# A hybrid decoder block: the second group of input columns on the shifted input, scale sums by a product with ones, later modulation queued behind

## The chip, the cores and the metric

The kernel runs on one core of a Trainium2 chip. The metric is the time on the device in microseconds (us) of one execution; lower is better. The engines of the core run side by side, each through its own queue in order, and wait for one another by semaphores: TensorE (PE, with its weight loads shown as PEld), VectorE (DVE), ScalarE (ACT), GpSimd (POOL) and SyncE (SP), which issues most of the loads. SBUF and PSUM are the memories on the chip.

## The reference

One layer of a decoder block on 512 positions of width 2048, in float32:

```python
mod = silu(c) @ w_ada + b_ada                      # 6 x 2048
shift1, scale1, gate1, shift2, scale2, gate2 = split(mod)
h = rms_norm(x, norm1_w) * (1 + scale1) + shift1
proj = h @ w_in                                    # 2048 x 7168
aq, ak, av, gq, gf, gi, gg = split(proj)           # 3 x 1024 for attention, 4 x 1024 for HGRN2
attn = rms_norm(dilated_attention(rope(rms_norm(aq)), rope(rms_norm(ak)), av), attn_out_norm_w)
f = lb + (1 - lb) * sigmoid(gf);  q = silu(gq) * 128 ** -0.5
hg = rms_norm(hgrn2(q, f, gi)) * silu(gg)
x = x + gate1 * (concat(attn, hg) @ w_out)
h2 = rms_norm(x, norm2_w) * (1 + scale2) + shift2
x = x + gate2 * (square(relu(h2 @ w_ff1)) @ w_ff2)
```

The case is about the first lines: the six modulation vectors are a product of one row with a matrix of 2048 x 12288, which has to be read from HBM in full, and nothing of `proj` can be finished before `scale1` and `shift1` are known.

## The kernel before

**Layout.** The width of 2048 is cut into 16 channel tiles of 128 (`NK`), the positions into four tiles of 128. The normalised input is kept transposed: `xnT[k]` holds channel tile k, 128 channels by 512 positions. For matmuls each operand is split into a high part, rounded to the matmul's format, and a low part with the rest: `hhi[k]`, `hlo[k]` for the input, `whi`, `wlo` for a weight tile (ACT makes the high part, DVE the low part, lines 35 to 41). A product is three matmuls: hi by whi, lo by whi, hi by wlo (`ch_mm` and `tok_mm`, lines 194 to 208).

**Modulation.** `gemv` (lines 116 to 131) computes a row of a vector-matrix product on DVE: it loads 16 slices of 128 channels, multiplies each by a column of the vector and adds it to one of two accumulators, even and odd slices apart. Each step of the generator is one load of 256 KB, with one slice of 512 columns or two slices of 256. What is left is a sum over the 128 partitions. `to_cols` (lines 138 to 152) does it by transposing each 128 columns of the accumulators on PE and adding up the transposed rows on ACT (a copy with an accumulated output), which gives the result as a column of 128 channels. With 512 columns the two accumulators are added first (line 143); with 256 both are transposed side by side. `mod_cols` (lines 160 to 170) adds the bias on DVE (line 167), and for a scale also forms `(scale + 1) * norm weight` (line 169).

**The first two column groups.** `first_groups` (lines 285 to 298) runs two channel tiles at a time and makes six blocks of 128 output columns: four of the forget gate f and two of the HGRN2 query. It is called for columns 4096 to 4607 with 3072 to 3327, and then for 4608 to 5119 with 3328 to 3583. In the first call `scale_block` computes the scale of the next two channel tiles (blocks of 256 columns) and then scales two tiles: `scaled` (lines 329 to 334) makes `xnT[k]` times `g1c`, from that its high part, from both the low part. The input is not shifted yet. Its shift is added afterwards, since (h + shift) @ w = h @ w + shift @ w: `shift_through` (lines 741 to 755) is one more `gemv`, of the shift vector with the weight columns, and adds the result to f or to the query as a bias. So both groups run on the scaled input alone. Beside the second group `shift_block` takes eight background steps per two tiles for the four shift blocks of 512 columns, and as soon as a block of four tiles has its shift, `shifted` (lines 336 to 339) puts it into `hhi`, `hlo` of these tiles, once the second group has read them. All later projections read the shifted input.

**Order.** The instructions of these stages are put in order when the program is built, for each engine: an instruction that is traced earlier goes first among those that are ready, by the builder's own estimate of time. `tc.issue_after(ins)` puts what a block traces on the engine of `ins` behind `ins` in that engine's queue; it binds no other engine, and no load on SP unless `ins` is on SP. From line 828 on, PE runs in the order of the program text (`manual_schedule`).

**After the two groups** come the projection of the HGRN2 values (line 830, `hv0`), during which the background steps of the two corrections at columns 4096 and 3072 run, and then the others. The queue `bgw` of background generators is: four shift blocks, the correction of f0, the correction of all four heads of `hq0`; then `later`: the correction of f1, the rows of gate1, and the scale and shift columns of the second modulation. `bg_step` advances the first generator in the queue by one step.

**Buffers.** Early loads and long-lived tiles share the pool `io` of 30 buffers (`slot`): x, `xnT`, the loads of the early `gemv`, and the copies of the results f and gq (`keep`, lines 733 to 739). PSUM has four banks with the tag `mm` and four with `bg`; the two query blocks of a group and the transposes of `to_cols` share the latter.

Of the kernel before, what the change touches and what calls it, by code (L numbers as in the profile page):

```python
# [8 lines left out]
F32 = mybir.dt.float32  # L9
# [6 lines left out]
P = 128  # L16
# [28 lines left out]
def hybrid_block(ctx, tc, x, c, positions, norm1_w, w_ada, b_ada, w_in, q_norm_w, k_norm_w,  # L45
# [28 lines left out]
    mhalf = const.tile([P, 32], F32, name="mhalf")  # L74
    pool.memset(mhalf, -0.5)

# [39 lines left out]
    def gemv(view, vec, col0, n=512, early=False):  # L116

        accs = [(work("acc") if early else gv.tile([P, 512], F32, name="acc"))[:, 0:n] for _ in range(2)]
        nk = 512 // n
        for k0 in range(0, NK, nk):  # L120
            raw = spare.pop(0) if early and spare else slot("araw") if early else gv.tile([P, 512], F32, name="araw", bufs=4)
            raw = raw.rearrange("p (k n) -> p k n", n=n)
            nc.sync.dma_start(raw, view[:, k0:k0 + nk, col0:col0 + n])
            for k in range(k0, k0 + nk):
                acc = accs[k % 2]
                if k < 2:
                    dve.tensor_scalar(acc, raw[:, k - k0], vec[:, k:k + 1], None, op0=ALU.mult)
                else:
                    dve.scalar_tensor_tensor(acc, raw[:, k - k0], vec[:, k:k + 1], acc, op0=ALU.mult, op1=ALU.add)  # L129
            yield  # L130
        gemv.acc = accs

    def run_all(g):
        for _ in g:
            pass
        return gemv.acc

    def to_cols(accs, dst):

        nb = accs[0].shape[1] // P  # L140
        parts = 1 if nb == 4 else 2
        if parts == 1:
            dve.tensor_tensor(accs[0], accs[0], accs[1], op=ALU.add)
        yield
        pc = bank("pc")
        for j in range(nb):
            for u in range(parts):
                c = (j * parts + u) * P
                pe.transpose(pc[:, c:c + P], accs[u][:, j * P:(j + 1) * P], ident)
        for j in range(nb):  # L150
            c = pc[:, j * parts * P:(j + 1) * parts * P]
            act.activation(c, c, AF.Copy, accum_out=dst[:, j:j + 1])

# [5 lines left out]

    def mod_cols(kind, b, dst, nw, n=512, early=False):  # L160

        for _ in gemv(ada_v, sc, kind * D + b * n, n, early):
            yield
        nb = n // P
        d = dst[:, b * nb:(b + 1) * nb]
        yield from to_cols(gemv.acc, d)
        dve.tensor_tensor(d, d, bcol[:, kind * NK + b * nb:kind * NK + (b + 1) * nb], op=ALU.add)
        if nw is not None:
            mod_cols.last = dve.scalar_tensor_tensor(d, d, 1.0, nw[:, b * nb:(b + 1) * nb], op0=ALU.add, op1=ALU.mult)
        yield  # L170
# [73 lines left out]

    first_scale = mod_cols(1, 0, g1c, n1c, 256, True)
    for _ in range(8):
# [18 lines left out]
    run_all(first_scale)  # L265
    second_scale = mod_cols(1, 1, g1c, n1c, 256, True)
    spare.extend(hp.tile([P, 512], F32, name="araw", tag=f"{c}{k}") for k in range(8, NK) for c in ("hi", "lo"))
# [32 lines left out]
    def scale_block(k0):  # L300
        if k0 == 0:
            run_all(second_scale)
        elif k0 < 14:
            run_all(mod_cols(1, k0 // 2 + 1, g1c, n1c, 256, True))
        for k in (k0, k0 + 1):
            scaled(k)

    def shift_start(k0):
        if k0 == 14:
            for _ in range(12):  # L310
                bg_step()

    shift_done, behind = set(), []

    def shift_gen(b):
        yield from mod_cols(0, b, s1c, None, 512, True)
        shift_done.add(b)

    def shift_block(k0):
        behind.extend((k0, k0 + 1))  # L320
        for _ in range(8):
            bg_step()
        while k0 == NK - 2 and len(shift_done) < 4:
            bg_step()
        for k in [k for k in behind if k // 4 in shift_done]:
            shifted(k)
            behind.remove(k)

    def scaled(k):
        for l, t in zip((hhi, hlo), pair(k)):  # L330
            l.append(t)
        act.activation(xnT[k], xnT[k], AF.Copy, scale=g1c[:, k:k + 1])
        act.copy(hhi[k], xnT[k])
        dve.tensor_tensor(hlo[k], xnT[k], hhi[k].bitcast(F32), op=ALU.subtract)

    def shifted(k):
        act.activation(hhi[k], xnT[k], AF.Identity, bias=s1c[:, k:k + 1])
        act.activation(xnT[k], xnT[k], AF.Identity, bias=s1c[:, k:k + 1])
        dve.tensor_tensor(hlo[k], xnT[k], hhi[k].bitcast(F32), op=ALU.subtract)

# [207 lines left out]
    def forget(hd, src, f, bias=0.0):  # L548
        act.activation(f, src, AF.Sigmoid, bias=bias)
        dve.tensor_scalar(f, f, omlb[:, hd:hd + 1], lb[:, hd:hd + 1], op0=ALU.mult, op1=ALU.add)  # L550

    def hgrn_q(ht):
        qb = project(3072 + ht * 512, ch_mm)
        qs = []
        for h in range(4):
            q = slot("gq")
            with tc.high_priority():
                act.copy(q, qb[h])
            qs.append(q)
        for q in qs:  # L560
            sg = wk.tile([P, 512], F32, name="sg", tag="ev", bufs=2)
            act.activation(sg, q, AF.Tanh, scale=0.5)
            dve.tensor_scalar(sg, sg, 0.5 * QS, 0.5 * QS, op0=ALU.mult, op1=ALU.add)
            dve.tensor_tensor(q, q, sg, op=ALU.mult)
        return qs
# [174 lines left out]

    def shift_through(col0):

        yield from gemv(win_v, s1c, col0, early=col0 < 4096 + 512)
        col = sm.tile([P, 8], F32, name="scol", bufs=2)
        yield from to_cols(gemv.acc, col[:, 0:4])
        for h in range(4):
            if col0 == 3072:
# [4 lines left out]
            else:  # L752
                f, hd = ((f0, h), (f1, 4 + h))[(col0 - 4096) // 512]
                forget(hd, f[h], f[h], col[:, h:h + 1])
# [76 lines left out]
    while bgw:  # L831
        bg_step()
    bgw[:] = later
    tasks.append(hgrn(f0, hq0, hv0, hrs[0]))
# [20 lines left out]
    def project_out(q, rate, after):  # L855
# [16 lines left out]
        return banks  # L872

    def nothing(i):
        pass

# [503 lines left out]
```

## Time and profile before

| what | us |
|---|---|
| median of three runs | 2305.67 |
| lowest and highest of the three | 2302.22, 2305.82 |
| the profiled execution | 2306.17 |
| its span in the profile | 2304.4 |
| matmuls (PE) busy | 2230.5 |
| VectorE busy | 1825.9 |
| ScalarE busy | 1103.0 |

The span is the time from the first to the last instruction that the profile shows; the execution's own time holds a little more. Busy times of engines overlap, so they don't add up to the span. Matmuls are pipelined: one lasts longer than the distance to the next one, and a PE that is busy throughout isn't always at its peak. A row of a timeline gives the start, the length and the engine of an instruction or of a few like ones in a row, its line, what it writes and reads and, in brackets, the idle time before it with what ended it. L12 is line 12 of the kernel.

### The profile page before, as it was taken

The page shows a single profiled execution, that of the slowest core. Times are in us where ns is not written, and L with a number is a line of the kernel's source. Part 1 is how long each engine was busy: PE and PEld are TensorE (multiplying, and loading weights), DVE is VectorE, ACT ScalarE, POOL GpSimd, SP SyncE. Part 2 cuts the span into 40 slices and gives each one's busy share as a digit, 9 for nine tenths or more (in the row PEclk, how much of TensorE's full clock was granted, in tenths as well). Part 3 has the DMA queues.
Part 4 walks back from the last instruction along what each step waited for, and adds up shares of the span by engine and source line. Part 5 has one row for each costly group of instructions (what it writes and reads, how often), then busy time and mean ns, then how long its engine had stood idle before and what let it go on. Part 6 is the DMA issues. An engine that isn't in the chain of part 4 may idle for free.

```text
span 2304.4 us, 33163 instructions
## 1 busy us (share of the span) xinstructions
PE 2230.5 (97%) x11769; PEld 1829.2 (79%) x11769; DVE 1825.9 (79%) x2773; ACT 1103.0 (48%) x1958; POOL 458.1 (20%) x668
## 2 busy tenths in 40 slices
PE   4999999999999999999999999999998999999999
PEld 3787877888778888888887888888887888888887
DVE  6899777677776565669767988988895789967878
ACT  5555434433344553457644555565563333344332
POOL 1000022000230000001332323323232222222221
PEclk9999999999999999999999999999999999999999
DMA  9798455556545256746999799889889987999784
GB/s 327 249 337 314 123 176 156 176 162 215 178 149 182 74 186 218 259 132 220 366 382 382 252 341 355 301 297 380 310 295 369 339 288 262 364 336 335 277 302 165
DMA packets 264695, 606.71 MB, mean 263 GB/s; under 512 B 23284, under 2 KB 44032, under 8 KB 264528
## 3 DMA queue, kind: packets, MB, share of 16 engines
q1 hardware_dynamic: 186800, 332.54, 42.8%
q0 software_dynamic: 72832, 262.60, 31.1%
q10 hardware_dynamic: 4896, 9.44, 1.2%
q8 instruction: 93, 1.52, 0.3%
q14 instruction: 74, 0.61, 0.1%
HBM read 522.68 MB, written 81.81 MB: 262 GB/s over the span
## 4 chain that ended last, share of the span: by engine, by line
PE 56%; DMA 16%; DVE 14%; issue 10%; POOL 2%; ACT 1%; SPq 0%; DVEq 0%; POOLq 0%; ACTq 0%
PE f L1160 9%; PE f L1161 9%; PE f L1159 9%; DMA araw<-in_w_ada_dram 7%; PE prj L198 4%; PE prj L200 4%; PE prj L199 4%; DMA f_lod<-fs 3%; DVE acc L129 3%; PE f L208 2%; PE f L206 2%; PE f L207 2%; DVE vlo L1146 2%; DVE wlo L40 2%; PE prj L206 2%
## 5 line engine op out<-in xcount | busy, mean ns | idle before, releaser
L1145 ACT CAST vhi<-raw 128x1024 fp32r<-128x1024 f32 x392 | 412.8, 1055 | 547.1 <-PE f L1161 434.3
L1146 DVE TENSOR_TENSOR vlo<-raw,vhi 128x1024 fp32r<-128x1024 f32 x392 | 477.4, 1225 | 154.3 <-ACT vhi L1145 153.5
L1159 PE MATMUL f<-vhi,Fh 128*128 128x512 f32 x1376 | 537.6, 391 | 8.3 <-DMA Fh<-h_hid 3.6
L1160 PE MATMUL f<-vlo,Fh 128*128 128x512 f32 x1376 | 538.1, 391 | 3.0 <-DVE vlo L1146 3.0
L1161 PE MATMUL f<-vhi,Fl 128*128 128x512 f32 x1376 | 537.2, 390 | 2.1 <-DMA Fl<-f_lod 1.3
L39 ACT CAST whi<-wraw 128x512 fp32r<-128x512 f32 (+1 forms) x368 | 219.8, 601 | 449.3 <-PE prj L200 323.7
L198 PE MATMUL prj<-whi,hi 128*128 128x512 f32 x896 | 365.0, 407 | 1.3 <-ACT gg L698 1.3
L200 PE MATMUL prj<-whi,lo 128*128 128x512 f32 x896 | 351.5, 392 | 0.0
L199 PE MATMUL prj<-wlo,hi 128*128 128x512 f32 x896 | 350.8, 391 | 0.0
L40 DVE TENSOR_TENSOR wlo<-wraw,whi 128x512 fp32r<-128x512 f32 (+1 forms) x368 | 245.1, 670 | 111.7 <-ACT whi L39 107.1
L129 DVE SCALAR_TENSOR_TENSOR acc<-araw,sc,acc 128x512 f32<-128x512 f32 (+1 forms) x392 | 253.9, 678 | 98.5 <-DMA araw<-in_w_ada_dram 97.2
L1159 PEld LDWEIGHTS f<-vhi,Fh 128*128 128x128 f32 x1376 | 259.0, 188 | 63.3 <-issue 7.1
L1160 PEld LDWEIGHTS f<-vlo,Fh 128*128 128x128 f32 x1376 | 259.0, 188 | 61.7 <-DVE vlo L1146 8.3
L1161 PEld LDWEIGHTS f<-vhi,Fl 128*128 128x128 f32 x1376 | 259.1, 188 | 56.7 <-DMA Fl<-f_lod 1.8
L1129 DVE TENSOR_TENSOR raw<-raw,raw 128x1024 f32<-128x1024 f32 x224 | 269.5, 1223 | 1.8 <-DMA raw<-in_w_ff_dram 1.5
L198 PEld LDWEIGHTS prj<-whi,hi 128*128 128x128 f32 x896 | 169.4, 189 | 36.5 <-ACT gg L698 1.6
L200 PEld LDWEIGHTS prj<-whi,lo 128*128 128x128 f32 x896 | 168.9, 188 | 36.8
L199 PEld LDWEIGHTS prj<-wlo,hi 128*128 128x128 f32 x896 | 169.6, 189 | 32.4 <-DVE wlo L40 0.4
L1097 POOL DMA_DIRECT2D Fh<-f_hid x112 | 80.9, 722 | 428.3 <-PE f L1161 414.8
L208 PE MATMUL f<-hi,wlo 128*128 128x512 f32 x256 | 99.8, 390 | 0.6 <-DVE wlo L40 0.6
L206 PE MATMUL f<-hi,whi 128*128 128x512 f32 x256 | 100.2, 391 | 0.0
L207 PE MATMUL f<-lo,whi 128*128 128x512 f32 x256 | 99.6, 389 | 0.0
(306 smaller groups left out, 2956.9 us busy)
## 6 DMA issues: line engine op xcount, KB each, us to landing
raw<-in_w_ff_dram SPq DMA_DIRECT2D x224, 512.0 KB, 10.0
araw<-in_w_ada_dram SPq DMA_DIRECT2D x384, 256.0 KB, 4.3
Fh<-f_hid POOLq DMA_DIRECT2D x112, 512.0 KB, 6.5
Fl<-f_lod POOLq DMA_DIRECT2D x112, 512.0 KB, 7.4
wraw<-in_w_in_dram SPq DMA_DIRECT2D x104, 512.0 KB, 4.1
Fh<-h_hid POOLq DMA_DIRECT2D x60, 512.0 KB, 6.8
Fl<-h_lod POOLq DMA_DIRECT2D x60, 512.0 KB, 8.3
f_hid<-part POOLq DMA_DIRECT2D x48, 512.0 KB, 8.1
```

The costliest lines, as they stand in the source:

```text
L39: nc.scalar.copy(hi, src)
L40: (eng or nc.vector).tensor_tensor(lo, src, hi.bitcast(F32), op=ALU.subtract)
L129: dve.scalar_tensor_tensor(acc, raw[:, k - k0], vec[:, k:k + 1], acc, op0=ALU.mult, op1=ALU.add)
L198: pe.matmul(banks[ti], lhsT=hi[:, ts], rhs=whi, start=first, stop=False)
L199: pe.matmul(banks[ti], lhsT=hi[:, ts], rhs=wlo, start=False, stop=False)
L200: pe.matmul(banks[ti], lhsT=lo[:, ts], rhs=whi, start=False, stop=last)
L1129: dve.tensor_tensor(dst, a, b, op=ALU.subtract)
L1145: act.copy(hi, src)
L1146: split_done.append(dve.tensor_tensor(lo, src, hi.bitcast(F32), op=ALU.subtract))
L1159: pe.matmul(banks[t], lhsT=fh[u][:, a, ts], rhs=whi[:, a], start=first, stop=False)
L1160: pe.matmul(banks[t], lhsT=fh[u][:, a, ts], rhs=wlo[:, a], start=False, stop=False)
L1161: pe.matmul(banks[t], lhsT=fl[u][:, a, ts], rhs=whi[:, a], start=False, stop=end)
```

## The change

There are three parts.

1. **Scale sums.** `scale_cols` takes the place of `mod_cols` for the first scale. The sum over the partitions is a matmul of each accumulator slice with a column of ones, the two accumulators added up in PSUM; ACT then forms `g1c = sum * n1c + b1c` in one instruction per tile, with `b1c = (bias + 1) * n1c` computed once at the start. `scaled` makes the high part from `xnT[k]` and `g1c` directly, and the scaled tile after it.
2. **The second group on the shifted input.** Before each fourth tile, `shift_block` runs background steps until the shift block of the next four tiles is there, and shifts these tiles; after every two tiles, `shift_next` runs nine background steps, queued on DVE behind the last addition of the two accumulators. The 16 loads and products of shift block 0 are started in the first group, eight after tile 13 and eight after tile 15 are scaled. f1 and the second half of the query need no correction any more; their activations follow at once. The correction at column 3072 is 256 columns wide instead of 512, and that at 4608 is gone.
3. **Later modulation.** Each step of the `later` generators is queued on DVE behind the last `shifted`. The small table work behind the first group (lines 761 to 819) is queued behind the last scale column.

```diff
-    pool.memset(mhalf, -0.5)
+    pool.memset(mhalf[:, 0:16], -0.5)
+    pool.memset(mhalf[:, 16:32], 1.0)
+    ones = mhalf[:, 16:17]
...
+    b1c = bcol[:, NK:2 * NK]
+    dve.scalar_tensor_tensor(b1c, b1c, 1.0, n1c, op0=ALU.add, op1=ALU.mult)
...
     def to_cols(accs, dst):
-        parts = 1 if nb == 4 else 2
-        if parts == 1:
-            dve.tensor_tensor(accs[0], accs[0], accs[1], op=ALU.add)
+        to_cols.last = dve.tensor_tensor(accs[0], accs[0], accs[1], op=ALU.add)
         yield
...
+    def scale_cols(b):
+        for _ in gemv(ada_v, sc, D + b * 256, 256, True):
+            yield
+        accs = gemv.acc
+        scale_cols.last_dve = gemv.last
+        pc = bank("pc")
+        for j in range(2):
+            for u in range(2):
+                pe.matmul(pc[:, j:j + 1], lhsT=accs[u][:, j * P:(j + 1) * P], rhs=ones, start=u == 0, stop=u == 1)
+        for j in range(2):
+            ks = slice(2 * b + j, 2 * b + j + 1)
+            scale_cols.last = act.activation(g1c[:, ks], pc[:, j:j + 1], AF.Identity, scale=n1c[:, ks],
+                                             bias=b1c[:, ks])
+        yield
...
         for k in (k0, k0 + 1):
             scaled(k)
+        if k0 >= 12:
+            with tc.issue_after(scaled.last.ins):
+                for _ in range(8):
+                    bg_step()
...
     def shift_block(k0):
-        behind.extend((k0, k0 + 1))
-        for _ in range(8):
-            bg_step()
-        while k0 == NK - 2 and len(shift_done) < 4:
-            bg_step()
-        for k in [k for k in behind if k // 4 in shift_done]:
-            shifted(k)
-            behind.remove(k)
+        if k0 % 4 == 0:
+            while k0 // 4 not in shift_done:
+                bg_step()
+            for k in range(k0, k0 + 4):
+                shifted(k)
+
+    def shift_next(k0):
+        with tc.issue_after(to_cols.last.ins):
+            for _ in range(9):
+                bg_step()
...
+        act.activation(hhi[k], xnT[k], AF.Copy, scale=g1c[:, k:k + 1])
         act.activation(xnT[k], xnT[k], AF.Copy, scale=g1c[:, k:k + 1])
-        act.copy(hhi[k], xnT[k])
-        dve.tensor_tensor(hlo[k], xnT[k], hhi[k].bitcast(F32), op=ALU.subtract)
+        scaled.last = dve.tensor_tensor(hlo[k], xnT[k], hhi[k].bitcast(F32), op=ALU.subtract)
...
-    bgw += [shift_through(4096), shift_through(3072)]
-    bt, bc = first_groups(4096, 3072, scale_block, shift_start)
+    bgw += [shift_through(4096, 512), shift_through(3072, 256)]
+    bt, bc = first_groups(4096, 3072, scale_block, nothing)
...
-    with tc.issue_after(mod_cols.last.ins):
+    with tc.issue_after(scale_cols.last.ins), tc.issue_after(scale_cols.last_dve.ins):
...
-    bt, bc = first_groups(4096 + 512, 3072 + 256, lambda k0: None, shift_block)
+    bt, bc = first_groups(4096 + 512, 3072 + 256, shift_block, shift_next)
     f1 = keep(bt, "f")
-    hq0 += keep(bc, "gq", QS)
-    later.insert(0, shift_through(4096 + 512))
+    for h in range(4):
+        forget(4 + h, f1[h], f1[h])
+    hq0 += keep(bc, "gq")
+    for q in hq0[2:]:
+        silu(q)
...
-    bgw[:] = later
+    def behind(steps, ins):
+        while True:
+            with tc.issue_after(ins):
+                if next(steps, steps) is steps:
+                    return
+            yield
+    bgw[:] = [behind(steps, shifted.last.ins) for steps in later]
```

`silu` is the code that `hgrn_q` had before, made into a function: a tanh on ACT and two instructions on DVE.

More of the change, by code (lines that the diff above doesn't have):

```diff
@@ L128, in gemv @@
                 else:
-                    dve.scalar_tensor_tensor(acc, raw[:, k - k0], vec[:, k:k + 1], acc, op0=ALU.mult, op1=ALU.add)
+                    gemv.last = dve.scalar_tensor_tensor(acc, raw[:, k - k0], vec[:, k:k + 1], acc, op0=ALU.mult,
+                                                         op1=ALU.add)
             yield
@@ L146, in to_cols @@
         for j in range(nb):
-            for u in range(parts):
-                c = (j * parts + u) * P
-                pe.transpose(pc[:, c:c + P], accs[u][:, j * P:(j + 1) * P], ident)
+            js = slice(j * P, (j + 1) * P)
+            pe.transpose(pc[:, js], accs[0][:, js], ident)
         for j in range(nb):
-            c = pc[:, j * parts * P:(j + 1) * parts * P]
-            act.activation(c, c, AF.Copy, accum_out=dst[:, j:j + 1])
+            js = slice(j * P, (j + 1) * P)
+            act.activation(pc[:, js], pc[:, js], AF.Copy, accum_out=dst[:, j:j + 1])
     g1c = const.tile([P, NK], F32, name="g1c")
@@ L168, in mod_cols @@
         if nw is not None:
-            mod_cols.last = dve.scalar_tensor_tensor(d, d, 1.0, nw[:, b * nb:(b + 1) * nb], op0=ALU.add, op1=ALU.mult)
+            dve.scalar_tensor_tensor(d, d, 1.0, nw[:, b * nb:(b + 1) * nb], op0=ALU.add, op1=ALU.mult)
         yield
@@ L242, in hybrid_block @@
     hhi, hlo, spare = [], [], []
-    first_scale = mod_cols(1, 0, g1c, n1c, 256, True)
+    first_scale = scale_cols(0)
     for _ in range(8):
@@ L265, in hybrid_block @@
     run_all(first_scale)
-    second_scale = mod_cols(1, 1, g1c, n1c, 256, True)
+    second_scale = scale_cols(1)
     spare.extend(hp.tile([P, 512], F32, name="araw", tag=f"{c}{k}") for k in range(8, NK) for c in ("hi", "lo"))
@@ L303, in scale_block, with nothing @@
         elif k0 < 14:
-            run_all(mod_cols(1, k0 // 2 + 1, g1c, n1c, 256, True))
+            run_all(scale_cols(k0 // 2 + 1))
         for k in (k0, k0 + 1):
             scaled(k)
-    def shift_start(k0):
-        if k0 == 14:
-            for _ in range(12):
-                bg_step()
-    shift_done, behind = set(), []
+        if k0 >= 12:
+            with tc.issue_after(scaled.last.ins):
+                for _ in range(8):
+                    bg_step()
+    def nothing(k0):
+        pass
+    shift_done = set()
     def shift_gen(b):
-        yield from mod_cols(0, b, s1c, None, 512, True)
+        yield from mod_cols(0, b, s1c, None, True)
         shift_done.add(b)
     def shift_block(k0):
-        behind.extend((k0, k0 + 1))
-        for _ in range(8):
-            bg_step()
-        while k0 == NK - 2 and len(shift_done) < 4:
-            bg_step()
-        for k in [k for k in behind if k // 4 in shift_done]:
-            shifted(k)
-            behind.remove(k)
+        if k0 % 4 == 0:
[7 more added lines that the diff above has]
+                bg_step()
     def scaled(k):
@@ L338, in shifted @@
         act.activation(xnT[k], xnT[k], AF.Identity, bias=s1c[:, k:k + 1])
-        dve.tensor_tensor(hlo[k], xnT[k], hhi[k].bitcast(F32), op=ALU.subtract)
+        shifted.last = dve.tensor_tensor(hlo[k], xnT[k], hhi[k].bitcast(F32), op=ALU.subtract)
     bgw = []
@@ L550, in forget, with silu @@
         dve.tensor_scalar(f, f, omlb[:, hd:hd + 1], lb[:, hd:hd + 1], op0=ALU.mult, op1=ALU.add)
+    def silu(q):
+        sg = wk.tile([P, 512], F32, name="sg", tag="ev", bufs=2)
+        act.activation(sg, q, AF.Tanh, scale=0.5)
+        dve.tensor_scalar(sg, sg, 0.5 * QS, 0.5 * QS, op0=ALU.mult, op1=ALU.add)
+        dve.tensor_tensor(q, q, sg, op=ALU.mult)
     def hgrn_q(ht):
@@ L560, in hgrn_q @@
         for q in qs:
[L561 to L564, printed above, removed]
+            silu(q)
         return qs
@@ L739, in keep, with shift_through @@
         return ts
-    def shift_through(col0):
-        yield from gemv(win_v, s1c, col0, early=col0 < 4096 + 512)
+    def shift_through(col0, n):
+        yield from gemv(win_v, s1c, col0, n, early=True)
         col = sm.tile([P, 8], F32, name="scol", bufs=2)
-        yield from to_cols(gemv.acc, col[:, 0:4])
-        for h in range(4):
+        nb = n // P
+        yield from to_cols(gemv.acc, col[:, 0:nb])
+        for h in range(nb):
             if col0 == 3072:
```

12 lines of the change are left out of this document (5 added, 7 removed).

## The prediction

> **What bounds the kernel now.** I read the shares by engine first, then busy time by stage, then the waits of TensorE (PE), and last the timelines of PE, VectorE (DVE), ScalarE (ACT) and the SP queue around each gap. In the stage rows the columns are the stretch, its length, the busy us (and instructions) of PE, PEld, DVE, ACT and POOL, the granted clock, the DMA share and GB/s.
>
> ```profile
> PE 2230.5 (97%) x11769; PEld 1829.2 (79%) x11769; DVE 1825.9 (79%) x2773; ACT 1103.0 (48%) x1958; POOL 458.1 (20%) x668
> ```
> ```profile
> 50.50:56.30 5.80, 3.83 (x12) 2.86 (x11) 5.80 (x18) 3.12 (x10) 0.00 (x0) 0.71 1.10 347
> ...
> 90.40:100.60 10.20, 6.15 (x15) 4.50 (x15) 10.20 (x24) 5.67 (x12) 0.00 (x0) 0.67 0.51 173
> 100.60:123.05 22.45, 22.45 (x101) 18.28 (x101) 15.41 (x55) 12.99 (x26) 0.00 (x0) 1.00 0.32 86
> 123.05:189.50 66.45, 66.44 (x298) 54.51 (x297) 64.24 (x116) 38.16 (x88) 4.75 (x8) 1.00 1.00 359
> ...
> 209.90:220.10 10.20, 5.34 (x16) 4.22 (x15) 9.80 (x18) 4.52 (x13) 0.00 (x0) 0.67 1.05 387
> 220.10:242.00 21.90, 21.90 (x98) 18.09 (x97) 15.51 (x28) 7.40 (x14) 0.00 (x0) 1.00 0.51 151
> ```
> ```profile
> 196.80 0.39 PE L199 MATMUL prj<-wlo,hi 128*128 128x512 f32 x1
> ...
> 199.07 0.39 PE L200 MATMUL prj<-whi,lo 128*128 128x512 f32 x1
> ```
>
> PE is busy 97% of the span, so time is won or lost only where PE waits or runs at a reduced clock. The first column group ends at 123.05, the second at about 189.5, and the projection of the HGRN2 values follows. Ten matmuls lie between the two starts of the last fence: 2.27 / 10 = 0.227 us each at full clock. The three short stages are those at a granted clock near 0.7. Their useful work is instructions times 0.227 us (0.114 for the four transposes of the third, half of whose 0.60 us below overlaps): 2.7, 3.4 and 3.2 us. So **3.1, 6.8 and 7.0 us are lost there, 16.9 in all**. The second group itself (123 to 189) loses nothing, with DVE busy 64 of 66 us and DMA full.
>
> ```profile
> 52.75 2.02 PE L206 MATMUL prj<-hi,whi 128*128 128x512 f32 x4 [1.97 <-ACT hi L333]
> ...
> 94.46 2.07 PE L206 MATMUL prj<-hi,whi 128*128 128x512 f32 x4 [4.05 <-ACT hi L333]
> ```
> ```profile
> PE pc L149 <- DVE acc L143: 4.9, 1, 4.9
> ```
> ```profile
> 86.63 0.20 ACT L152 ACTIVATION_READ_ACCUMULATOR pc<-pc 128x1 f32 x1
> ...
> 92.57 1.33 ACT L332 ACTIVATE xnT<-xnT,g1c 128x512 f32<-128x512 f32 x2 [1.14 <-DVE g1c L169]
> ```
> ```profile
> 88.84 0.17 DVE L167 TENSOR_TENSOR g1c<-g1c,bcol 128x2 f32<-128x2 f32 x1
> ...
> 92.36 0.17 DVE L169 SCALAR_TENSOR_TENSOR g1c<-g1c,n1c 128x2 f32<-128x2 f32 x1
> ...
> 95.42 1.16 DVE L129 SCALAR_TENSOR_TENSOR acc<-araw,sc,acc 128x512 f32<-128x512 f32 x2
> ```
>
> The reader sees why the first two gaps open. The column sums of a scale block are in hand at 86.8 (86.63 + 0.20), but two tiny DVE instructions finish them, and these stand in DVE's queue behind products of later blocks: 92.53 instead of about 87. PE waits 4.1 us for hi. The third gap is PE standing at the transposes of a shift correction until DVE has added it up (4.9 us).
>
> **The change part by part.** *Scale sums.* Per block of two tiles, four matmuls with a column of ones replace four transposes, and two one-column activations replace two reductions and two DVE instructions; ACT writes g1c itself.
>
> ```profile
> L149 PEld LDWEIGHTS pc<-ident,acc x128: 137/140/230, 15.7 to 1059.0; 128*128 128x128 f32 x128
> ```
> ```profile
> 116.29 0.22 ACT L779 ACTIVATE lbe<-lbe 128x16 f32<-128x16 f32 x1 [0.20 <-DVE lbe L778]
> ```
>
> A matmul of one column isn't in the trace: between nothing and the weight load of the transpose it replaces, 0.14 us, so four of them take 0 to 0.56 us against 0.45; I take no difference. The one-column activation lies between nothing and the 0.22 us row; two of them. The scaled tile's hi no longer waits for the scaled copy either. At the two gaps g1c would be there 4 to 5 us earlier, so the 3.1 and 6.8 us should go. The 16 wide products of shift block 0 also queue behind the last scaled tiles now, instead of among them (the row at 95.42 is two of these), while DVE is full in both stages. Next to be late is the scale of tiles 10 and 11:
>
> ```profile
> 85.32 0.49 PE L149 MATMUL pc<-ident,acc 128*128 128x128 f32 x3
> ```
>
> PE would come to tile 10 at 50.2 + 4 x (36 x 0.227 + 0.45) = 84.7 (tile 2 at 50.2, where the first gap opens), but the products of this block end at about 85, and hi is ready some 1.2 us later. I charge 1.4 us. **Gain in the first group: 9.9 - 1.4 = 8.5 us**, its end near 114.5; bounds 5 (the slower pace of a full DVE) and 10.
>
> *Second group on the shifted input.* The correction for f1 (16 loads, 16 products, four transposes) and half of that for hq0 vanish. They lay under PE's cover: in 220 to 242 DVE is busy 15.5 of 21.9 us. I count only six transposes of 0.114 us, 0.7. The shift is applied before the value projection, and the shift correction that PE stood at is issued a group earlier: **7.0 us gained**. The remaining correction for hq0 has eight loads, and its transposes are fixed five tiles, 5 x 12 x 0.227 = 13.6 us, into the value projection, enough cover. f1's sigmoids and the two tanhs go to ACT, busy 7.4 of 21.9 us there; nothing. Queueing the later modulation behind the last shifted tile costs nothing while PE has its own work; without that cover its first products, 0.67 us each (below), would come late one by one.
>
> *The wait it adds.* The second group starts four tiles at a time, each four behind: add, four transposes on PE, four reductions on ACT, one bias add on DVE, hi on ACT. PE works its queue in order, and the traced place of these transposes is behind the matmuls of the previous four tiles. In the profile of before the transposes of shift block 2, placed behind six pairs of tiles, run just there: 123.05 + 6 x 36 x 0.227 + 2 x 0.45 = 173.0, the second row below. Nothing else is left for PE then, as all later matmuls need shifted tiles. The same chain, run in before without anybody waiting:
>
> ```profile
> 134.18 0.60 PE L149 MATMUL pc<-ident,acc 128*128 128x128 f32 x4
> ...
> 173.00 0.60 PE L149 MATMUL pc<-ident,acc 128*128 128x128 f32 x4
> ```
> ```profile
> 138.36 1.95 ACT L337 ACTIVATE hi<-xnT,s1c 128x512 fp32r<-128x512 f32 x3 [1.58 <-DVE s1c L167]
> ...
> 175.88 2.57 ACT L337 ACTIVATE hi<-xnT,s1c 128x512 fp32r<-128x512 f32 x4 [0.51 <-DVE s1c L167]
> ```
>
> From the transposes to the first hi it took 138.36 - 134.18 + 1.95/3 = 4.8 us and 175.88 - 173.00 + 2.57/4 = 3.5. Less the transposes' 0.5 that is 3.0 to 4.3 us idle; I take 3.3, near the shorter, since part of the longer is DVE's queue, which is less full when PE waits. Then the clock: beyond the waits themselves the stages above lost 3.1 - 2.0, 6.8 - 4.1 and 7.0 - 4.9 us, that is 1.1 (after the wait of 2.0 us), 2.7 and 2.1. I take 1.9. **Each border costs 5.2 us (bounds 3.0 and 7.0), four of them 20.8.**
>
> The Trainium skill speaks to this ("TensorE: Matmul & The Clock Gate", section "Why this matters for your kernels"): gaps of PE over about 3 us bring the half clock back. By that, gaps of just 3 us might keep the full clock. This trace already shows 0.71 after 2.0 us, so the row decides for me; by the page the borders would cost 3.3 each and the sum would be some 8 us lower.
>
> *Can DVE and DMA keep that pace?*
>
> ```profile
> 203.27 4.72 DVE L129 SCALAR_TENSOR_TENSOR acc<-araw,s1c,acc 128x512 f32<-128x512 f32 x7
> ```
> ```profile
> L40 DVE TENSOR_TENSOR wlo<-wraw,whi 128x512 fp32r<-128x512 f32 x14 | 9.7, 702 | 0.0
> ...
> L339 DVE TENSOR_TENSOR lo<-xnT,hi 128x512 fp32r<-128x512 f32 x12 | 8.1, 699 | 0.0
> ...
> L40 DVE TENSOR_TENSOR wlo<-wraw,whi 128x256 fp32r<-128x256 f32 x15 | 6.3, 430 | 0.4 <-ACT whi L39 0.4
> ```
> ```profile
> 90.47 30.29 SPq L189 DMA_DIRECT2D wraw<-in_w_in_dram  x7
> 120.81 9.72 SPq L123 DMA_DIRECT2D araw<-in_w_ada_dram  x13
> ```
> ```profile
> 119.87 1.96 ACT L737 ACTIVATE f<-prj 128x512 f32<-128x512 f32 x3 [0.23 <-PE prj L208]
> ```
>
> Per four tiles DVE has 17 x 0.67 + 4 x (0.70 + 0.43) + 4 x 0.70 = 18.7 us, about 17 where neighbours overlap; PE has 72 x 0.227 = 16.3, and 21.5 with its border. DMA has 16 x 0.26 + 1.57 = 5.8 MB, 16.1 us at 359 GB/s. So both fit inside 21.5 but hardly inside 16.3. The last rows tell when block 1 can start to load: the loads that the program places behind the copies of the first group's results went out at 120.81, with the first such copy at 119.87, though DMA's share was 0.32 in that stage. In the changed kernel the loads of shift blocks 1 to 3 stand behind those copies.
>
> **Sum.** - 8.5 - 7.0 - 0.7 + 20.8 = + 4.6 us on the profiled execution's 2306.17 (span 2304.4, 1.8 around it): **2311 us**, the median of the runs being 2305.67. What follows is bound by PE as before and moves along.
>
> **Rivals.**
> 1. *Borders at part of the price* (not slower). Either the clock stays up, or the transposes of two borders slip ahead of matmuls.
>
> ```profile
> 114.42 0.27 PE L765 MATMUL ps_v<-ident,rows 128*128 128x128 f32 x1
> ```
>
> For it: this transpose, placed behind the first group, runs 8 us before the group's end, so readiness can overrule place, and DVE may have the shift's sum 4 us early (17 against 21.5). Against: it went ahead where the next tiles' scale was late, and within a block nothing is late. Borders of 10 to 13 us in all: - 3 to - 6, 2302. This is also the time by the page's rule.
> 2. *Borders nearly free*: all transposes run early and the chain lies under the last matmuls. The first border stays (the copies hold ACT and the banks), and the second waits for loads begun at 114.5: 5.2 + 2 against 16.2, 2297, or 2290 with neither. Against: DVE at 17 us in 16.3.
> 3. *Loads or DVE take over*: if a block's products start only when the tiles before are shifted, a block lasts 17 + 5.2 + the first landing, some 25 us instead of 21.5: + 3.5 each for three blocks, 2321. It decides when DMA falls under 5.8 MB / 21.5 us = 270 GB/s; the stage ran at 359.
> That the change doesn't do what it says would show as no shifted reads ahead of the second group; its code leaves no room for it.
>
> **Chances.** Forecast 0.46 (own range 2305 to 2317), rival 1 0.30, rival 2 0.14, rival 3 0.10. A measurement tells 0.2%, 4.6 us, from no change. The forecast lies on that edge: 0.26 slower, 0.19 same, 0.01 faster. Rival 1: 0.16 faster, 0.13 same, 0.01 slower. With the others: faster 0.31, same 0.32, slower 0.37. For 8 in 10 the range is 2292 to 2318: it leaves out the far end of rival 2 and the upper half of rival 3.
>
> **What would show it.** First group: no wait of hi on g1c above 2 us, end at 112 to 117. Borders: four waits of PE for hi of a shifted tile, 3 to 4 us each, clock near 0.7 behind each. Value projection: no wait at a transpose. Were the waits at the borders under 1 us, or the transposes found in the midst of a block's matmuls, the sum is wrong by what they spare; were PE waiting for a sum of products instead of hi, rival 3 holds.

## The result, and the profile after

| | before | after |
|---|---|---|
| median, us | 2305.74 (4 runs, 2302.22 to 2309.98) | 2325.87 (4 runs, 2324.81 to 2333.83) |
| ratio, 95% interval | | 1.0088 [1.0069, 1.0107] |
| profiled execution, us | 2306.17 | 2325.36 |
| its span, us | 2304.4 | 2323.6 |
| first group ends, us | 123.05 | 115.33 |
| second group lasts, us | 66.45 | 90.67 |
| from there to the first product of HGRN2 (pA), us | 58.9 | 62.1 |
| first product of HGRN2 at, us | 248.38 | 268.13 |

The changed kernel is 0.9% slower, 20 us. The forecast of 2311 (2292 to 2318) had the side right and the size wrong. On the spans the difference is 19.2 us. The first group gives - 7.7 us, the second + 24.2, the value projection behind it + 3.2, all that follows - 0.5. So the difference between these two executions arises in the first 270 us.

The shares by engine, and then the stages of the changed kernel (columns as in the prediction: stretch, length, busy time of PE, PEld, DVE, ACT and POOL, granted clock, DMA share, GB/s):

```profile
PE 2235.8 (96%) x11795; PEld 1833.5 (79%) x11795; DVE 1811.9 (78%) x2741; ACT 1099.4 (47%) x1930; POOL 455.4 (20%) x669
```
```profile
50.50:56.30 5.80, 5.80 (x31) 4.88 (x31) 5.67 (x14) 4.90 (x11) 0.00 (x0) 1.00 1.10 349
90.40:100.60 10.20, 10.19 (x50) 8.48 (x51) 10.20 (x23) 6.93 (x15) 0.00 (x0) 1.00 0.87 287
100.60:115.33 14.73, 14.73 (x66) 11.93 (x65) 12.93 (x30) 7.22 (x12) 0.00 (x0) 1.00 0.35 96
...
120.17:130.00 9.83, 9.58 (x31) 7.27 (x32) 7.39 (x18) 7.16 (x12) 4.17 (x8) 0.74 0.73 246
...
146.22:156.00 9.78, 8.88 (x32) 6.79 (x33) 9.78 (x16) 5.48 (x9) 0.00 (x0) 0.85 1.06 384
...
170.15:180.00 9.85, 9.01 (x34) 7.13 (x35) 9.85 (x18) 7.97 (x19) 0.71 (x1) 0.85 0.62 220
...
222.30:246.00 23.70, 15.68 (x62) 12.77 (x62) 17.30 (x40) 5.07 (x11) 0.00 (x0) 0.86 0.39 111
```

The first two rows are the stages in which before stood still: 31 and 50 matmuls where there were 12 and 15, at full clock. The rows after 120 are new: three stretches at a clock of 0.74 to 0.85 in the second group, and the value projection, which before lost 7.0 us in its gap, loses more: 62 matmuls in 23.70 us, where 62 x 0.227 = 14.1 would do.

What PE waited for in the changed kernel between 110 and 205 us (total, times, longest), and its timeline:

```profile
PE prj L224 <- ACT hi L360: 11.2, 3, 4.4
PE pc L151 <- DVE acc L146: 3.0, 1, 3.0
PE prj L225 <- DVE lo L362: 2.0, 3, 0.9
```
```profile
115.33 0.60 PE L151 MATMUL pc<-ident,acc 128*128 128x128 f32 x4
120.17 2.07 PE L224 MATMUL prj<-hi,whi 128*128 128x512 f32 x4 [4.24 <-ACT hi L360]
...
142.50 1.11 PE L151 MATMUL pc<-ident,acc 128*128 128x128 f32 x4 [2.95 <-DVE acc L146]
146.22 2.08 PE L224 MATMUL prj<-hi,whi 128*128 128x512 f32 x4 [2.61 <-ACT hi L360]
...
165.16 0.60 PE L151 MATMUL pc<-ident,acc 128*128 128x128 f32 x4
170.15 2.08 PE L224 MATMUL prj<-hi,whi 128*128 128x512 f32 x4 [4.39 <-ACT hi L360]
172.88 0.72 PE L151 MATMUL pc<-ident,acc 128*128 128x128 f32 x4
...
230.48 0.69 PE L151 MATMUL pc<-ident,acc 128*128 128x128 f32 x2 [8.02 <-DVE acc L146]
```

There are three borders that cost something, not four. The transposes of the last shift block (172.88) run amid the matmuls of the block before. The three waits for hi (11.2), the one for the sum (3.0) and those for lo (2.0) make 16.2 us; the other 8.0 of the 24.2 are slow clock and small rests. The last row is the largest single wait, and it is in the value projection: the transposes of the correction at column 3072.

Why these sums are late, on DVE, and then on SP's queue with the first copies of the second group's results on ACT, in the changed kernel:

```profile
126.99 1.06 DVE L131 TENSOR_SCALAR acc<-araw,sc 128x512 f32<-128x512 f32 x2
...
141.76 0.68 DVE L146 TENSOR_TENSOR acc<-acc 128x512 f32<-128x512 f32 x1
...
156.63 0.68 DVE L146 TENSOR_TENSOR acc<-acc 128x512 f32<-128x512 f32 x1
...
186.94 0.87 DVE L131 TENSOR_SCALAR acc<-araw,sc 128x512 f32<-128x512 f32 x2
...
215.23 0.88 DVE L133 SCALAR_TENSOR_TENSOR acc<-araw,s1c,acc 128x256 f32<-128x256 f32 x2
...
230.00 0.42 DVE L146 TENSOR_TENSOR acc<-acc 128x256 f32<-128x256 f32 x1
```
```profile
170.98 1.12 SPq L127 DMA_DIRECT2D araw<-in_w_in_dram  x2
...
202.23 5.86 SPq L127 DMA_DIRECT2D araw<-in_w_ada_dram  x4
208.37 0.38 SPq L207 DMA_DIRECT2D wraw<-in_w_in_dram  x1
210.66 0.33 SPq L127 DMA_DIRECT2D araw<-in_w_ada_dram  x1
211.03 3.50 SPq L127 DMA_DIRECT2D araw<-in_w_in_dram  x7
```
```profile
202.81 1.28 ACT L764 ACTIVATE f<-prj 128x512 f32<-128x512 f32 x2 [0.51 <-PE prj L226]
```

The products of shift block 1 start at 126.99, when the lo of the tiles before are done, and are added up at 141.76, after PE's last matmul ahead of their border (139.15). Block 2 is added up at 156.63, 8 us before its transposes run (165.16): this border is a matter of place. Of the correction's eight loads the first goes out near 172, and the other seven at 211.03. In the program they stand behind the copies, of which the first run at 202.81; on SP loads of the later modulation (in_w_ada, the rows at 202.23 and 210.66) stand ahead of them as well. Those have four buffers of their own, and the five of them from 202.23 on take SP until 210.99. On DVE the later modulation starts at 186.94, ahead of the correction's products (215.23 to 229.97). From 215.23 to the sum at 230.00 DVE works without a break, but little of it is the correction. What it did between 215.2 and 230.5:

```profile
L133 DVE SCALAR_TENSOR_TENSOR acc<-araw,s1c,acc 128x256 f32<-128x256 f32 x14 | 6.4, 478 | 0.0
L40 DVE TENSOR_TENSOR wlo<-wraw,whi 128x512 fp32r<-128x512 f32 x5 | 3.4, 683 | 0.0
L573 DVE TENSOR_SCALAR f<-f,omlb,lb 128x512 f32<-128x512 f32 x5 | 2.6, 541 | 0.0
L133 DVE SCALAR_TENSOR_TENSOR acc<-araw,sc,acc 128x512 f32<-128x512 f32 x2 | 1.5, 742 | 0.0
L580 DVE TENSOR_TENSOR gq<-gq,sg 128x512 f32<-128x512 f32 x2 | 1.4, 685 | 0.0
L579 DVE TENSOR_SCALAR sg<-sg 128x512 f32<-128x512 f32 x2 | 0.8, 422 | 0.0
```

The correction's products take 6.4 us, the low parts of the projection's weights 3.4, the gates (L573, L579, L580) 4.8 and the later modulation 1.5.

### The profile page after: what moved, and what is told of

It reads as the page before. It is cut to its first block, busy times and chain, and to the rows that moved or that the text cites. A ratio compares the mean times of both kernels' runs of the same rounds, so it can differ in the third digit from the quotient of the medians.

```text
span 2323.6 us, 33124 instructions
## 1 busy us (share of the span) xinstructions
PE 2235.8 (96%) x11795; PEld 1833.5 (79%) x11795; DVE 1811.9 (78%) x2741; ACT 1099.4 (47%) x1930; POOL 455.4 (20%) x669
## 4 chain that ended last, share of the span: by engine, by line
PE 62%; DVE 15%; DMA 14%; issue 6%; ACT 2%; POOL 1%; SPq 0%; DVEq 0%; ACTq 0%; POOLq 0%
PE f L1195 11%; PE f L1196 11%; PE f L1194 10%; DMA araw<-in_w_ada_dram 8%; PE prj L216 5%; PE prj L217 5%; PE prj L218 5%; DVE acc L133 3%; DMA Fl<-h_lod 3%; DVE vlo L1181 2%; PE f L226 2%; PE f L224 2%; PE f L225 2%; DVE wlo L40 2%; DVE raw L1164 2%
```

## The experiments

The kernel before was timed beside each; ratios are to it, with 95% intervals. "pA" is the start of the first product of HGRN2 in the profiled execution, 248.38 before and 268.13 after. What follows pA lasted 2054 to 2066 us in the profiled executions (2055.5 in the changed kernel's), and some of them are the longest of their kernel: that of experiment 2 took 2326.33 us, the others there 2313.95 to 2317.52. So pA tells of what lies ahead of it, and the totals go by all executions of a kernel.

**1. One part at a time.** The scale part alone, on the kernel before; and the changed kernel with the scale sums as before:

```diff
+    first_scale = scale_cols(0)          # before, with all of part 1
...
-    first_scale = scale_cols(0)          # after, with part 1 undone
+    first_scale = mod_scale(0)           # four transposes, two reductions, two DVE instructions
```

> The kernel before with the first part of the change alone: scale sums by a product with ones, and the high part made from g1c directly; the second group stays on the unshifted input. Theory 1 (the first group is held up by the tiny VectorE instructions behind other products, and nothing later holds it back): the first group ends near 115 instead of 123, and the whole is 7 to 8 us faster than before, about 2298. Rival (VectorE and the loads set the pace up to the value projection): the gain is given back at the wait for the correction's transposes in the value projection, which grows from 4.9 to 10 us or more, and the whole is within 2 us of before.

> The changed kernel with its first part undone: the scale sums by transposes, with the bias and the factor added by VectorE, as before; the rest as changed. If the parts add up, the loss of the second part is 20 + 8 = 28 us, about 2334, the first group ends near 123 and the second lasts 90 us. Rival: the borders of the second group are set by loads and VectorE, not by the end of the first group; then part of the 8 us is hidden there, and the whole is under 2330.

Scale part alone: 0.9992 [0.9978, 1.0006] (10 runs), pA 242.37. Without it: 1.0113 [1.0096, 1.013], pA 272.11, which lies between the two expectations (2334 us would be a ratio of 1.012, 2330 us one of 1.0105) and doesn't tell them apart. So the loss belongs to parts 2 and 3. The scale part wins 6.0 us up to pA, but its total can't be told from no change. That is the rival's total, but not its cause: the wait at the correction's transposes is 4.9 us, as before. The profile shows one place that takes the gain back. ScalarE's queue late in the kernel, first before, then with the scale part alone:

```profile
1763.78 8.44 ACTq L1276 DMA_DIRECT2D d<-x1d  x8
1772.26 3.90 ACT L1145 CAST vhi<-raw 128x1024 fp32r<-128x1024 f32 x4 [8.39 <-DMA Fl<-f_lod]
```
```profile
1757.04 15.07 ACTq L1297 DMA_DIRECT2D d<-x1d  x8
1772.15 3.88 ACT L1166 CAST vhi<-raw 128x1024 fp32r<-128x1024 f32 x4 [15.02 <-DMA d<-x1d]
```

The eight reads of x1d begin 6.7 us earlier and end at the same time, 1772, in a stretch in which the DMA engines are busy throughout (share 1.02 to 1.04 from 1725 to 1775). PE waits 8.6 us for vhi there instead of 2.0. That is one profile of each. In the two kernels of experiment 8, which have the second group as before too, these reads begin at 1763.41 and 1767.12 and end at 1772.71 and 1773.85: over 10 us their end hardly follows their start. What sets the end is open; that it is the full DMA was not tried by itself.

**2. The correction at column 3072 ahead of the copies.**

```diff
     bt, bc = first_groups(4096 + 512, 3072 + 256, shift_block, shift_next)
+    while bgw:
+        bg_step()
     f1 = keep(bt, "f")
```

> The changed kernel, with all steps of the correction at column 3072 traced ahead of the copies of the second group's results, instead of in the value projection. Theory 1 (the loads of this correction wait for buffers behind these copies, and PE for them): its loads go out before the copies, the wait of 8.0 us at the correction's transposes and the slow clock behind it vanish, and the whole is 9 to 11 us faster than the changed kernel, about 2315. Rival (VectorE is late because the products of the later modulation and the gates' instructions stand ahead): the loads go out earlier, but the wait only moves, and the whole gains less than 4 us.

1.0045 [1.0026, 1.0065], by the ratios about 10 us below the changed kernel, as the first theory said; pA 258.52. All eight loads go out together now (the ninth of the row belongs to the correction before), and PE has no wait between 206 and 250. SP's queue:

```profile
170.96 6.49 SPq L127 DMA_DIRECT2D araw<-in_w_in_dram  x9
```

So the 8 us wait comes from the place of the correction's steps behind the second group. The edit moves its loads and its products together, ahead of the copies, the gates and the later modulation, and doesn't say which of them counts. The second group ends 3 us later; its DVE has these products to do as well now.

**3. The later modulation behind the correction** instead of behind the last shifted tile.

```diff
-    bgw[:] = [behind(steps, shifted.last.ins) for steps in later]
+    bgw[:] = [behind(steps, to_cols.last.ins) for steps in later]
```

> The changed kernel, with the products of the later modulation queued on VectorE behind the last addition of the correction at column 3072, instead of behind the last shifted tile. Theory 1 (the loads of the correction are late): it still waits for its loads, issued at about 211, and the wait of 8.0 us shrinks only by the later products between 215 and 230, some 3 of them, 2 us. Rival (the later products on VectorE are what makes it late): the wait falls under 3 us and the whole is 6 to 8 us faster than the changed kernel.

1.0065 [1.0045, 1.0086], some 5 us lower by the ratios, though the intervals overlap; pA 263.09. The wait at the transposes shrinks from 8.0 to 3.8 us (the changed order, PE and SP's queue):

```profile
225.71 0.55 PE L151 MATMUL pc<-ident,acc 128*128 128x128 f32 x2 [3.80 <-DVE acc L146]
```
```profile
205.82 3.63 SPq L127 DMA_DIRECT2D araw<-in_w_in_dram  x7
```

The seven loads did not stay at 211, as the first theory had it: with the later modulation out of their way on SP they go out 5.2 us earlier, 1.3 us after the first copies (204.55) and ahead of the copies of the query (210.12 and 211.10). From their first product (210.72) to the sum (225.23) DVE takes 14.5 us, where it took 14.8 with the modulation's products in between. So what was won came with the loads, and hardly by the products that ran ahead. Earlier loads alone are not enough either: in the kernel of experiment 5 they go out at 207.53, 3.5 us earlier than in the changed kernel, DVE takes 16.2 us from their first product (213.52) to the sum (229.74), and PE still waits 8.75 us.

**4. The place of the transposes.** All 18 steps of the next shift block behind the first pair of tiles, alone and with edit 2:

```diff
     def shift_next(k0):
         with tc.issue_after(to_cols.last.ins):
-            for _ in range(9):
+            for _ in range(18 if k0 % 4 == 0 else 0):
                 bg_step()
```

> The steps of the next shift block are all traced behind the first pair of tiles of the present block, instead of nine behind each of its two pairs, so that its transposes come to stand amid the present block's matmuls. Theory 1 (a border costs 8 us because the transposes stand behind the last matmul and the chain to hi follows them with nothing for PE to do): the border of about 8 us ahead of the third four tiles goes, total about 8 us below the changed kernel, ratio 1.005. Rival (the border is the pace of loads and VectorE, whose sums come that late anyway): PE waits for the sum at the moved transposes instead, total within 3 us of the changed kernel or above it, ratio 1.008 to 1.011.

> Both edits: the steps of the next shift block behind the first pair of tiles, and the rest of the correction at column 3072 traced ahead of the copies of the second group. Theory 1: their gains add, about 10 + 8 us below the changed kernel, ratio 1.001. Rival (borders are the pace of loads and VectorE): as with the early correction alone, ratio 1.0045.

Alone: 1.0071 [1.0052, 1.009], pA 265.31. With edit 2: 1.0038 [1.0023, 1.0054], pA 255.43, nearer to the rival's 1.0045 than to 1.001. The place moves as meant, and the third border shrinks, but not to nothing (alone, PE):

```profile
160.52 0.60 PE L151 MATMUL pc<-ident,acc 128*128 128x128 f32 x4
167.41 1.20 PE L224 MATMUL prj<-hi,whi 128*128 128x512 f32 x4 [1.02 <-ACT hi L360]
171.24 0.50 PE L225 MATMUL prj<-lo,whi 128*128 128x512 f32 x1 [2.18 <-DVE lo L362]
```

The wait for hi falls from 4.39 to 1.02 us and that for lo grows from 0.84 to 2.18, while DVE is busy throughout (10.00 of 10 us from 165 to 175). PE waits for no sum at the moved transposes, which the rival expected. Some 3 us at pA came of it where 8 were expected, in both pairs; in the totals the intervals overlap. So neither theory holds as it stood.

**5. PE kept busy at the borders.**

```diff
-            pe.transpose(pc[:, js], accs[0][:, js], ident)
+            to_cols.last_pe = pe.transpose(pc[:, js], accs[0][:, js], ident)
...
     def shift_gen(b):
         yield from mod_cols(0, b, s1c, None, True)
+        pd = bank("pd")
+        with tc.issue_after(to_cols.last_pe.ins):
+            for j in range(20):
+                c = (j % 4) * P
+                pe.transpose(pd[:, c:c + P], ident, ident)
```

> The changed kernel with 20 more transposes of the identity (2.3 us, read by nobody) behind the transposes of each shift block, where PE stands idle. Theory 1 (part of each border is the granted clock near 0.7 to 0.85 in the 10 us behind it; by matmuls counted there 1.6 to 2.5 us a border, 6 in all): the clock stays at 1.0 behind the borders and the total falls by 4 to 6 us, ratio 1.006 to 1.007. Rival (the low clock follows from something else than PE's idle time, or PE merely waits that much longer for the next lo): no change, ratio 1.009.

1.0073 [1.0059, 1.0087], by the ratios 3.5 us below the changed kernel, with intervals that overlap; but up to pA (267.38) only 0.75 us are won where 4 to 6 were expected. The stretches behind the three borders, as shown above for the changed kernel:

```profile
120.17:130.00 9.83, 9.22 (x27) 6.86 (x28) 7.39 (x18) 7.23 (x13) 4.09 (x8) 0.65 0.77 248
...
146.22:156.00 9.78, 8.00 (x27) 6.16 (x26) 9.78 (x17) 6.26 (x10) 0.00 (x0) 0.74 1.06 386
...
170.15:180.00 9.85, 9.09 (x53) 7.49 (x51) 9.82 (x17) 8.60 (x20) 0.71 (x1) 1.00 0.60 214
```

At the third border only 0.43 us of idle time were left, and the clock stayed at 1.00 (0.85 in the changed kernel). At the first 2.05 us were left and at the second 2.61 before the transposes, and the clock fell to 0.65 and 0.74. That speaks for the idle time as the cause of the slow clock; only the third border shows it saved.

**6. Less work for VectorE.** Every second wlo of the second group on Pool, on the changed kernel and on that of the pair in 4:

```diff
-            wt = load_w(win_v, k0, c_f, ahead=False)
-            wc = load_w(win_v, k0, c_q, 256, None, ahead=False)
+            wt = load_w(win_v, k0, c_f, eng=eng, ahead=False)
+            wc = load_w(win_v, k0, c_q, 256, eng, ahead=False)
...
-    bt, bc = first_groups(4096 + 512, 3072 + 256, shift_block, shift_next)
+    bt, bc = first_groups(4096 + 512, 3072 + 256, shift_block, shift_next, pool)
```

> The changed kernel with every second subtraction for wlo in the second group on Pool instead of VectorE (2.2 us of VectorE's time less in each four tiles; Pool is idle there). Theory 1 (VectorE, busy 30.5 of 30.6 us from 139.55 to 170.15, sets the time of the sums and of lo, and so part of the borders): PE's wait for the sum at the second border shrinks from 3.0 us to under 1, those for lo with it, total 3 to 5 us below the changed kernel, ratio 1.007. Rival (the place of the transposes alone sets the borders): total within 2 us of the changed kernel, ratio 1.008 to 1.009. Pool's subtraction of 128x512 has no row so far: were it over 2 us, PE would wait for wlo and the total be above the changed kernel.

> The kernel with the moved transposes and the early correction, and every second wlo of the second group on Pool. Theory 1 (with the transposes moved, VectorE is what is left of the borders): 4 to 8 us below that kernel without Pool, ratio 1.000 to 1.002. Rival (what is left is the chain to hi and the slow clock): ratio 1.003 to 1.004.

1.0128 [1.0115, 1.0142] and 1.0082 [1.0067, 1.0097]: some 9 and 10 us slower than without Pool, which is the last case of the expectation, though the subtraction takes 1.74 us and not over 2. The two theories aren't told apart by it. A subtraction on Pool, and two rows of DVE in the first of these kernels, one without Pool at work and one beside it:

```profile
158.34 1.74 POOL L40 TENSOR_TENSOR wlo<-wraw,whi 128x512 fp32r<-128x512 f32 x1 [17.09 <-DVE acc L131]
```
```profile
145.09 2.74 DVE L133 SCALAR_TENSOR_TENSOR acc<-araw,sc,acc 128x512 f32<-128x512 f32 x4
...
158.19 2.44 DVE L133 SCALAR_TENSOR_TENSOR acc<-araw,sc,acc 128x512 f32<-128x512 f32 x2
```

Four products take 2.74 us by themselves, and two take 2.44 while Pool works. Over the group the mean product goes from 747 to 854 ns, and DVE wins nothing. The Trainium skill says so ("Perfetto Trace Analysis", section "Optimizing Scalar/DVE Operations": offloading between GpSimd and DVE may not help because they share an SBUF read port); the trace agrees with the outcome, and that the port is the reason no run here shows. The second group lasts 98.9 us instead of 90.7 in the first of these kernels: PE's waits in it are 19.6 us instead of 16.2, and over the ten us behind its second and third border the clock is 0.55 and 0.54 instead of 0.85.

**7. Half the products of shift blocks 1 to 3.** The kernel leaves out the other half of these sums, with their loads.

```diff
         for k0 in range(0, NK, nk):
+            if k0 >= nuse:                 # 8 for shift blocks 1 to 3, else 16
+                yield
+                continue
```

> The changed kernel with only the first 8 of 16 loads and products of shift blocks 1 to 3 (the other half of these sums is left out); steps, tiles and matmuls of the second group as before. VectorE has 5.4 us and DMA 2.1 MB less to do in each four tiles. Theory 1 (full VectorE and its order cost most of the second and third border: sums late by 3 us, lo late, transposes placed late): the second group lasts 75 to 80 us instead of 90.8, PE waits for no sum, total 10 to 15 us below the changed kernel, ratio 1.002 to 1.004. Rival (the chain from transposes to hi and the slow clock behind it, whatever VectorE has to do): PE waits for hi at three borders as before, the second group lasts 86 us or more, ratio 1.006 to 1.008.

1.004 [1.0023, 1.0057], pA 259.29. The total is where the first theory put it, the second group is not: it lasts 87.9 us (115.15 to 203.09), as the rival said. PE in it:

```profile
140.17 0.60 PE L154 MATMUL pc<-ident,acc 128*128 128x128 f32 x4
142.01 0.66 PE L154 MATMUL pc<-ident,acc 128*128 128x128 f32 x4 [1.25 <-DVE acc L149]
146.91 2.07 PE L227 MATMUL prj<-hi,whi 128*128 128x512 f32 x4 [4.24 <-ACT hi L363]
...
153.26 0.50 PE L228 MATMUL prj<-lo,whi 128*128 128x512 f32 x1 [2.56 <-DVE lo L365]
```

The transposes of two blocks now stand one behind the other at 140 to 142.7, one border is gone, and the other has its chain of 4.2 us and the wait for lo. So with 5.4 us of DVE's work and 2.1 MB of loads less in each four tiles only 3 us of the group's extra 24 go. Of the 21.5 that are left 12.9 are PE's waits, and the clock over the ten us behind the two borders is 0.66 and 0.67. What was won, 5.9 us more, lies behind the group, where the seven loads go out at 204.48 and DVE comes to the correction earlier (the wait there is 3.8 us instead of 8.0).

**8. More out of the scale part.** The wait of 4.9 us that it leaves in the value projection, attacked by stepping the background work more slowly, at 1.5 a tile; and at 1.85 with the later modulation behind the correction's sum:

```diff
-    hv0 = evac(project(5120, tok_mm, 2.0), "gi")
+    hv0 = evac(project(5120, tok_mm, 1.5), "gi")       # or 1.85
...
-    bgw[:] = later                                     # with 1.85 only
+    bgw[:] = later[:1] + [behind(steps, to_cols.last.ins) for steps in later[1:]]
```

> The kernel before with the scale part alone, and the value projection stepping its background work at 1.5 a tile instead of 2, so that the transposes of its correction stand later. Theory 1 (what is won early reaches the end): the wait of 4.9 us at these transposes and the slow clock behind it go, some 7 us below the scale part alone, 2300, ratio 0.996 to 0.997. Rival (a place late in the kernel, where eight reads of x1d hold ScalarE's queue until 1772 us in both, takes it back): first product of HGRN2 some 12 us earlier than before, PE's wait for vhi near 1772 grown to 13 us or more, ratio 0.998 to 1.000.

> The kernel before with the scale part alone, the later modulation queued behind the add of the correction at column 3072 and the value projection stepping at 1.85 a tile, so that the transposes stand one tile (12 matmuls, 2.7 us) later and three of VectorE's products (some 2 us) no longer stand ahead of the sum. Theory 1: the wait of 4.9 us and the slow clock behind it go, first product of HGRN2 near 236 us, and the gain reaches the end: ratio 0.995 to 0.997. Rival (the place near 1772 us, where eight reads of x1d hold ScalarE's queue, or another late one takes it back): first product near 236, ratio 0.998 to 1.000.

1.0005 [0.9992, 1.0018] with pA 247.60, and 1.0032 [1.002, 1.0044] with pA 242.87. Neither reached the 236 us on which both theories rested, so they don't tell them apart. In the first the wait moves to the end of the projection and is 9.7 us; in the second two are left, and the postponed modulation meets HGRN2 (its profile, PE's waits between 250 and 420):

```profile
PE pB L592 <- DVE z L619: 6.7, 1, 6.7
```

No version beat the kernel before; the scale part alone can't be told from it.

## Why the prediction was wrong, step by step

- **First group, 8.5 us: right.** 7.7 were measured, both gaps at full clock. That this gain reaches the end is another matter: beside the other parts 4.0 us of it are left at pA (272.11 to 268.13; the intervals of 1.0113 and 1.0088 overlap), and on the kernel before 6.0 us at pA and nothing that can be measured at the end (experiment 1).
- **"The remaining correction for hq0 has eight loads, and its transposes are fixed five tiles, 5 x 12 x 0.227 = 13.6 us, into the value projection, enough cover": this step failed**, and with it the 7.0 us gained and the 0.7 for the transposes. The stage cost 3.2 us more instead of 7.7 less: 10.9 of the 14.6 us by which the sum of + 4.6 missed the span's + 19.2. The cover was counted from the first matmul of the projection, but the loads weren't there to start with, and DVE had other work between them and the sum. Seven of the eight went out at 211.03, 5 us into the stage, behind the second group's copies in the program and behind the later modulation on SP; from their first product to the sum DVE took 14.8 us, and only 6.4 of these are the correction's products. PE came to the transposes at 222.5 and stood 8.0 us. The prediction reads the place behind the copies from the first group and applies it to the shift blocks alone; and it prices the gates at nothing, as work for ACT, while their DVE instructions (f0's among them) are 4.8 of the 14.8 us. Experiment 2 moves the correction's steps ahead of all this and wins 10 us. How much each of these obstacles is worth by itself stays open.
- **"Queueing the later modulation behind the last shifted tile costs nothing while PE has its own work": wrong**, and part of the same wait. The last shifted tile is before the correction, so the queue order lets the modulation ahead of it, and on SP, which the order doesn't bind, its loads stand ahead of the seven. Experiment 3 takes the wait from 8.0 to 3.8 us, by loads that go out 5.2 us earlier.
- **Borders, four at 5.2 us: the mechanism was right, the term mis-sized.** Three at 8.1 us, 24.2 instead of 20.8. Per border: 3.7 us for hi (3.3 predicted), 0.7 for lo and 1.0 for the sum (neither was counted), and 2.7 of slow clock and rests (1.9 predicted). The fourth is free because its transposes slipped into the block before, as rival 1 said of two of them. This term makes 3.4 of the 14.6 us, and the first group 0.8; what follows pA takes 0.5 off.
- **Rival 3** (products that start only when the tiles before are shifted; PE waiting for a sum instead of hi) came true at one border: the blocks lasted 26.05 us (120.17 to 146.22) and 23.93 us, where it said 25. But neither place (experiment 4, some 3 us at pA) nor half of DVE's work (experiment 7, 3 us in the group) gives the 24 us back. In both the next link of the chain takes over: hi, lo, and the clock behind what is left.
- **The clock** fell behind all three borders, as forecast, but less: 0.74, 0.85 and 0.85 over the ten us behind them, where it was put near 0.7. The range's lower half, which hung on a cheaper border, found no support.
- **Range.** The errors of the sum's three large terms had one sign, and no case held a loss in the value projection: a cover was taken as given, and so its failure had no place in the bounds.

## What to carry to other kernels

Before work is called covered, follow its first load through the queue that issues it: the cover counts from there, not from where the consumer starts. A queue order that names one instruction to stand behind has to name the last one that matters, or what is postponed overtakes what is urgent; and it has to hold for the loads too, as work that is postponed on one engine can still stand ahead in the queue that issues the loads. And when a chain is put on the critical path several times, price all its links at once (sum, hi, lo, clock): shortening one only shows the next.

## What was not expected of the hardware

- With an idle PE of 2.05 us, the granted clock was 0.65 in the ten us behind it, which hold another 0.55 us of waiting; with 0.43 us left it stayed at 1.00 (experiment 5).
- Pool's subtraction of 128x512 took 1.74 us, and two of DVE's products beside it took 2.44 us, where four by themselves take 2.74 (experiment 6).
- Four f32 products with a column of ones are eight matmul records of 0.95 us in all, where the four transposes that they replace show 0.60. The prediction took no difference; over eight blocks it is at most 3 us.

```profile
97.57 0.95 PE L171 MATMUL pc<-mhalf,acc 128*128 128x1 f32 x8
```
